# The front end of an encoder kernel is rebuilt: adaLN weights first, tokens turned with scale and shift, twelve early products, one schedule up to the sweeps

## The chip, the cores and the metric

The kernel runs on one core of a Trainium2 chip. A core has five engines: TensorE (PE in the profile) multiplies, VectorE (DVE), ScalarE (ACT) and GpSimd (POOL) do the elementwise work, SyncE (SP) issues transfers. Each engine runs its own instructions in the order in which they were written, and semaphores hold it until what it needs is there. The metric is the time of one execution on the device in microseconds (us), lower is better.

## What is computed

One layer of a hybrid encoder, in float32, on a prompt of 1024 tokens and a sample of 256, each of 1024 features. The 1280 tokens are handled together.

```
def mixer_layer(x, c, w_ada, b_ada, norm_g, w_in, ...):
    mod = c @ w_ada + b_ada                                  # adaLN: c is one row for each sequence
    shift, scale, gate = jnp.split(mod[:, None, :], 3, axis=-1)
    h = rms_norm(x, norm_g) * (1.0 + scale) + shift
    p = h @ w_in                                             # 1024 -> 11280 columns
    cb, cc, cx, cz, q, k, v, o, mz, gpre, gmerge = split_combined(p)
    y_conv = cb * centred_dwconv3(cc * cx, conv_w, conv_b) * jax.nn.silu(cz)
    ...                                                      # two chunkwise mLSTM passes give hm
    y_m = jax.nn.sigmoid(o) * hm * jax.nn.silu(mz)
    g_conv, g_mlstm = jnp.split(jax.nn.sigmoid(gmerge), 2, axis=-1)
    merged = g_conv * (y_conv @ w_proj_conv) + g_mlstm * (y_m @ w_proj_mlstm)
    return x + gate * (merged @ w_out)
```

## The kernel before, in words

**Stages.** The kernel has four: a front end that brings x and the adaLN weights in and makes h with features on the partitions; the long product h @ w_in; the mLSTM sweeps; the merge and the output product. The change is in the first two.

**Front end** (L336 to L458). SP loads eight small tables (L242 to L267), the ten chunks of x of 128 tokens (`xin`, 0.5 MB each), then eight pieces of the adaLN weights (`wa`, 1 MB each) through five buffers, and the first weights of the long product. ACT squares and sums each chunk, DVE makes the inverse root by Newton's steps and scales the chunk by it. PE turns the chunks (80 turns of 128x128, L392), and ACT and DVE alternately copy the results into 16 tiles `xt` of 128 features by 640 tokens. PE multiplies c by the weights (32 matmuls of 4x512, L405, each run as two passes), the result is turned and becomes `s1` and `shf`, a scale and a shift for each feature and sequence (L440). This part is one plan of its own, and its pools are closed behind it. Then `affine` (L849) applies scale and shift to the xt tiles in place.

**The long product.** h is cut into four quarters: B11 and B21 are the lower and the upper half of the features for the first 640 tokens, B12 and B22 for the others. A `Strassen` group takes two times 128 columns of w_in and makes the four results in seven products instead of eight (L527): against B11 (`b00` in the profile), B21 (`b10`), t2, t3, t1 and t4 (in `xt` buffers), B22 (`b11`). Here t3 = B22 - B12, t2 = t3 + B11, t1 = B12 - B11, t4 = B21 - t2, made once by `combine` (L843). Every operand is held as two parts: a rounded high part (ACT's cast) and the rest as low part (a subtraction on DVE or POOL), by `both_parts` (L834) for h and `split_op` (L325) for weights. A product is then high by high, high by low, low by high: 24 matmuls of 128x320, for each of four feature quarters 6. It goes to one of three accumulators (`psX`), from which ACT or DVE adds it to a partial result in a buffer `q` of 640 columns (L606, L618). There are 44 groups, 308 products: 8 groups for the merge gates, 3 for head 0, 8 for the output gates, 16 for the convolution, 9 for the other heads. The first two products of a group need only B11 and B21; in four groups these two, called corners, are made first (`Corner`), while the other operands are still in the making.

**Order.** Nothing is run as it is written down. `op` records each step with its engine, a cost, what it reads and writes and a step number; `Board.order` (L95) sets the order of all recorded steps by letting each engine take the step that can start first, with ties within 0.25 us broken by step number. A step can't be placed before a buffer of its pool is free, and buffers of one kind are given out in the order in which they were recorded. `play` then writes the instructions down. Before the change that happens in several plans, one for each `phase`: the front end; the gates and head 0; the first output gates with the recurrences (`recurrences`, the running maxima and decays of the mLSTM gates, with pool `gt`); the other output gates with the exponentials (`weights`, pool `gw`); the convolution (pool `ab`); the other heads with the adaLN third (`thirds`, pool `gw2`). The ring of q buffers is made anew: eight in the gate plan, five in the middle plans, six in the last. A pool that opens where an older one lay waits until that one's last readers, stores included, are done.

Of the kernel before, what the change touches and what calls it, by code (L numbers as in the profile page):

```python
# [40 lines left out]
class Board:  # L41
# [30 lines left out]
    def op(self, eng, us, f, r=(), w=(), after=(), low=False):  # L72
# [16 lines left out]
        o.bufs = {b for t in (*r, *w) for b in (t if isinstance(t, tuple) else (t,)) if isinstance(b, self.Buf)}  # L89
# [5 lines left out]
    def order(self):  # L95
# [4 lines left out]
        for o in self.ops:  # L100
            o.before = {b for b in o.before if not b.played}
            count[o] = len(o.before)
            for b in o.before:
                after.setdefault(b, []).append(o)
# [25 lines left out]
        while ready:  # L130
            first = None
            can = []
            for o in ready:
                t = begin(o)
                if t is not None:
                    can.append((t, o))
                    if first is None or t < first[0]:
                        first = t, o
# [42 lines left out]
def encoder_kernel(  # L181
# [39 lines left out]
    v_dr = dram.tile([T, D], F32, name="v_dr")  # L221

# [19 lines left out]
    dma(rows[0:8, :], c_prompt.rearrange("a (r p) -> (a r) p", p=P))  # L242
    dma(rows[8:16, :], c_sample.rearrange("a (r p) -> (a r) p", p=P))
    dma(rows[RSH:RSH + 16, :], b_ada[0, 0:2 * D].rearrange("(r p) -> r p", p=P))
    dma(rows[RNG:RNG + 8, :], norm_g.rearrange("a (r p) -> (a r) p", p=P))
    dma(rows[RMH:RMH + 8, :], mh_norm_g.rearrange("a (r p) -> (a r) p", p=P))
    dma(rows[RCW:RCW + 24, :], conv_w.rearrange("a w (r p) -> (a w r) p", p=P))
    dma(rows[RCB:RCB + 8, :], conv_b.rearrange("a (r p) -> (a r) p", p=P))
# [18 lines left out]
    dma(b32[0:16, :], b_gates.rearrange("a s h -> (a s h)").rearrange("(x o) -> x o", o=1))  # L267

    def rsqrt_newton(pool, out, v, n):

        r = pool.tile([P, n], F32, tag="rs_r", name="rs_r")
        t = pool.tile([P, n], F32, tag="rs_t", name="rs_t")
        A.activation(r[:], v, AF.Sqrt, bias=zero[:, 0:1], scale=1.0)
        V.reciprocal(r[:], r[:])
        V.tensor_tensor(out=t[:], in0=r[:], in1=r[:], op=ALU.mult)
        V.tensor_tensor(out=t[:], in0=t[:], in1=v, op=ALU.mult)
        V.tensor_scalar(out=t[:], in0=t[:], scalar1=-0.5, scalar2=1.5, op0=ALU.mult, op1=ALU.add)
        V.tensor_tensor(out=out, in0=t[:], in1=r[:], op=ALU.mult)
# [34 lines left out]
    xp = xstack.enter_context(tc.tile_pool(name="xp", bufs=17))  # L313
    lo_, hi_ = slice(0, TH2), slice(TH2, T)
# [17 lines left out]
    raw_a = {}  # L332

    def corner_split(n, j):
        raw = raw_a[n]
        w = split_op(lambda: raw[:].rearrange("p a (b c) -> p (a b) c", b=2)[:, 4 * j:4 * j + 4, :], [raw])  # L336
        for b in w:
            b.open = True
        raw.open = j == 0
        return w  # L340


    xt = {jl: [buf(xp, [P, TH2], F32, "xt", 17) for _ in range(4)] for jl in ((0, 0), (1, 0), (0, 1), (1, 1))}
    GROUPS = [range(0, 3), range(3, 5), range(5, 8), range(8, 10)]

    with tc.tile_pool(name="xs", bufs=1) as xs, tc.tile_pool(name="ad", bufs=1, side="right") as ad, \
            tc.tile_pool(name="psP", bufs=1, space=PSUM) as psP:
        rst, ssq = (xs.tile([P, NC], F32, name=nm) for nm in ("rst", "ssq"))
        junk = xs.tile([P, D], F32, name="junk")
        xin = [buf(xs, [P, D], F32, "xin", 10) for _ in range(NC)]  # L350
        was = [buf(ad, [P, 2 * D], F32, "wa", 5) for _ in range(KT)]
        pada = [psP.tile([P, 2, 512], F32, name=f"pada{h}") for h in range(2)]
        cz4 = ad.tile([P, KT, 4], F32, name="cz4")
        mod = ad.tile([4, 2 * D], F32, name="mod")
        modT = ad.tile([P, 2, KT, 2], F32, name="modT")

        def load_x(cs):
            for c in cs:
                load(512, lambda c=c: xin[c][:], x_rows(c), (), [xin[c]])

        def norm_x(cs):
            n, s = len(cs), slice(cs[0], cs[-1] + 1)
            sq = [("ssq", c) for c in cs]
            for c in cs:
                op("ACT", 1.35, lambda c=c: A.activation(junk[:], xin[c][:], AF.Square, bias=zero[:, 0:1], scale=1.0,
                                                         accum_out=ssq[:, c:c + 1]), r=[xin[c]], w=["junk", ("ssq", c)])
            op("DVE", .2, lambda: V.tensor_scalar(out=ssq[:, s], in0=ssq[:, s], scalar1=1.0 / D, scalar2=EPS, op0=ALU.mult,
                                                  op1=ALU.add), r=sq, w=sq)
            r, t = (buf(xs, [P, n], F32, f"{nm}{cs[0]}", 1) for nm in ("rr", "rt"))
            op("ACT", .3, lambda: A.activation(r[:], ssq[:, s], AF.Sqrt, bias=zero[:, 0:1], scale=1.0), r=sq, w=[r])  # L370
# [8 lines left out]
            op("DVE", 1.0, newton, r=[*sq, r], w=[r, t, ("rst", cs[0])])  # L379
            for c in cs:  # L380
                op("DVE", .75, lambda c=c: V.tensor_scalar(out=xin[c][:], in0=xin[c][:], scalar1=rst[:, c:c + 1], scalar2=None,
                                                           op0=ALU.mult), r=[xin[c], ("rst", cs[0])], w=[xin[c]])

        def turn_x(i, cs):
            t0, tn = cs[0] * P, len(cs) * P
            for kt in range(KT):
                px = buf(psP, [P, 512], F32, "px", 2)
                dst, d0 = xt[kt // 4, t0 // TH2][kt % 4], t0 % TH2
# [1406 lines left out]
```

## Time and profile before

| | us |
|---|---|
| median of 3 runs (1753.81 to 1754.83) | 1753.84 |
| the profiled execution | 1753.36 |
| its span, first to last instruction | 1751.6 |
| PE busy (96%) | 1686.7 |
| DVE busy (55%) | 957.3 |
| ACT busy (35%) | 611.3 |
| POOL busy (40%) | 693.9 |

In the page's picture of the span in 40 slices, PE is at 5 and 9 tenths in the first two slices of 44 us, at 6 in the third (88 to 131 us), and at 9 or more nearly everywhere behind. Matmuls overlap, so their busy times add up to more than the time between their starts; for the time a product takes, starts are counted instead. The profiled execution's time is 1.76 us longer than its span.

### The profile page before, as it was taken

How to read it: one execution, taken by the hardware profiler on the slowest of the kernel's cores; microseconds unless marked ns; L12 is line 12 of the kernel's file. 1: busy time of each engine (PE TensorE's matmuls, PEld its weight loads, DVE VectorE, ACT ScalarE, POOL GpSimd, SP SyncE). 2: the span in 40 equal slices, each digit the busy share in tenths (PEclk: the TensorE clock that was granted, in tenths of full speed). 3: DMA queues.
4: the chain of work that ended last, by engine and by line, in shares of the span. 5: the costliest groups of instructions: out<-in, count | busy, mean ns of one | idle time of the engine just before them, and what ended most of it. 6: DMA issues, size and time to landing. Idle time of an engine off the chain costs nothing.

```text
span 1751.6 us, 27967 instructions
## 1 busy us (share of the span) xinstructions
PE 1686.7 (96%) x10702; PEld 1596.3 (91%) x10702; DVE 957.3 (55%) x1653; ACT 611.3 (35%) x1201; POOL 693.9 (40%) x511
## 2 busy tenths in 40 slices
PE   5969999999999999999999999999999999999997
PEld 2569999999999999999999999999888889898986
DVE  4496343345564556555565666552147777565645
ACT  5443333223553222222222222222246565433222
POOL 0264333233674466766666533333210001223412
PEclk9979999999999999999999999999999999999999
DMA  8213233221663222112221344335878864684531
GB/s 303 91 59 132 98 101 101 88 80 45 176 180 104 64 79 79 63 56 71 71 67 67 118 137 136 112 121 197 292 238 268 268 219 153 228 278 132 216 120 60
DMA packets 213754, 239.53 MB, mean 137 GB/s; under 512 B 12420, under 2 KB 172404, under 8 KB 212596
## 3 DMA queue, kind: packets, MB, share of 16 engines
q1 hardware_dynamic: 213620, 237.74, 42.0%
q8 instruction: 85, 1.39, 0.3%
q14 instruction: 49, 0.40, 0.1%
HBM read 169.46 MB, written 68.23 MB: 136 GB/s over the span
## 4 chain that ended last, share of the span: by engine, by line
PE 88%; DVE 5%; DMA 3%; issue 2%; ACT 1%; SPq 1%; POOL 0%; DVEq 0%; ACTq 0%; POOLq 0%
PE acc L675 58%; PE qc L1296 3%; PE u L1314 3%; PE accd L1469 2%; PE accd L1470 2%; PE accd L1471 2%; PE accd L1682 2%; PE accd L1683 2%; PE accd L1681 2%; PE pada L405 2%; PE acc L1537 2%; PE acc L1536 2%; PE acc L1538 2%; DVE xt L846 1%; PE misc L810 1%
## 5 line engine op out<-in xcount | busy, mean ns | idle before, releaser
L606 DVE TENSOR_TENSOR q<-acc,q 128x640 f32<-128x640 f32 x292 | 236.7, 821 | 337.0 <-PE acc L675 333.0
L329 POOL TENSOR_TENSOR wl<-comb,wh 128x512 fp32r<-128x512 f32 x176 | 240.6, 1369 | 303.1 <-ACT wh L328 274.1
L329 POOL TENSOR_TENSOR wl<-raw,wh 128x512 fp32r<-128x512 f32 x136 | 182.2, 1340 | 249.2 <-ACT wh L328 246.1
L675 PE MATMUL acc<-xt,wh 128*128 128x320 f32 x1408 | 265.7, 311 | 1.2 <-POOL xt L841 1.2
L675 PEld LDWEIGHTS acc<-xt,wh 128*128 128x128 f32 x1408 | 221.8, 189 | 1.7 <-POOL xt L841 1.4
L328 ACT CAST wh<-comb 128x512 fp32r<-128x512 f32 x176 | 108.5, 619 | 209.7 <-PE acc L675 188.8
L328 ACT CAST wh<-raw 128x512 fp32r<-128x512 f32 x136 | 83.9, 620 | 272.6 <-PE acc L675 214.0
L675 PE MATMUL acc<-xt,wl 128*128 128x320 f32 x704 | 161.1, 310 | 0.0
L1497 POOL TENSOR_TENSOR wl<-raw,wh 128x512 fp32r<-128x512 f32 x28 | 36.4, 1301 | 234.0 <-ACT wh L1496 233.5
L675 PEld LDWEIGHTS acc<-xt,wl 128*128 128x128 f32 x704 | 118.2, 189 | 0.1
L495 ACT ACTIVATE q<-q,zero 128x640 f32<-128x640 f32 x80 | 66.4, 830 | 90.4 <-DVE q L606 87.8
L559 DVE TENSOR_TENSOR comb<-raw 128x512 f32<-128x512 f32 x88 | 78.8, 896 | 31.1 <-DMA raw<-in_w_in_dram 19.8
L675 PE MATMUL acc<-t2H,wh 128*128 128x320 f32 x352 | 83.1, 318 | 8.4 <-ACT t2H L840 7.2
L675 PE MATMUL acc<-t2L,wh 128*128 128x320 f32 x352 | 82.4, 316 | 5.1 <-DVE t2L L841 5.1
L675 PE MATMUL acc<-t2H,wl 128*128 128x320 f32 x352 | 82.4, 316 | 4.0 <-POOL wl L329 4.0
L559 DVE TENSOR_TENSOR comb<-raw,comb 128x512 f32<-128x512 f32 x44 | 46.0, 1045 | 72.5 <-POOL wl L329 72.5
L675 PE MATMUL acc<-b00H,wh 128*128 128x320 f32 x352 | 81.5, 313 | 2.2 <-ACT b00H L840 2.2
L675 PE MATMUL acc<-b11H,wh 128*128 128x320 f32 x352 | 81.8, 313 | 0.6 <-DVE q L606 0.6
L1469 PE MATMUL accd<-y,wh 128*128 128x320 f32 x256 | 79.5, 310 | 2.8 <-DVE og L1447 1.5
L675 PE MATMUL acc<-b00L,wh 128*128 128x320 f32 x352 | 81.0, 311 | 0.3 <-DVE b00L L841 0.3
L675 PE MATMUL acc<-b10H,wh 128*128 128x320 f32 x352 | 80.9, 311 | 0.0
L675 PE MATMUL acc<-t3H,wh 128*128 128x320 f32 x352 | 80.7, 311 | 0.0
(281 smaller groups left out, 4188.9 us busy)
## 6 DMA issues: line engine op xcount, KB each, us to landing
raw<-in_w_in_dram SPq DMA_DIRECT2D x96, 256.0 KB
raw<-in_w_in_dram SPq DMA_DIRECT2D x44, 512.0 KB
th_dr<-q SPq DMA_DIRECT2D x32, 320.0 KB
th<-th_dr SPq DMA_DIRECT2D x32, 320.0 KB
wa<-in_w_ada_dram SPq DMA_DIRECT2D x8, 1024.0 KB
raw<-in_w_proj_conv_dram SPq DMA_DIRECT2D x16, 512.0 KB
k<-kn_dr SPq DMA_DIRECT2D x64, 128.0 KB
raw<-in_w_proj_mlstm_dram SPq DMA_DIRECT2D x16, 512.0 KB
```

The lines of the kernel that those rows point to most:

```text
L328: op("ACT", .63, lambda: A.copy(wh[:], src()), r=r, w=[wh])
L329: op("POOL", 1.4, lambda: G.tensor_tensor(out=wl[:], in0=src(), in1=fp(wh[:]), op=ALU.subtract), r=[*r, wh], w=[wl])
L405: op("PE", .88, lambda h=h, j=j: PE.matmul(pada[h][0:4, j, :], cz4[:, kt, :], was[kt][:, h * D + j * 512:h * D + (j + 1) * 512], start=kt ...
L495: A.activation(out, in_, AF.Tanh, bias=zero[:, 0:1], scale=0.5)
L559: op("DVE", .9, lambda: V.tensor_tensor(out=t[:], in0=x(), in1=y(), op=o), r=[x.tok, y.tok], w=[t])
L606: op("DVE", .82, lambda: V.tensor_tensor(out=two(dst()), in0=acc[:, :, 0:TQ], in1=two(t()), op=ALU.add), r=[acc, t.tok], w=[dst.tok])
L675: PE.matmul(acc[:, q, 0:TQ], st_[:, k_, :], m_[:, q * TQ:(q + 1) * TQ], start=k_ == 0 and n == 0, stop=k_ == 3 and n == 2)
L1296: PE.matmul(pq[:, 0:HD + 2], qTs[i][:, kd, c * P:(c + 1) * P], C[:, kd, :], start=kd == 0, stop=kd == 1)
L1314: PE.matmul(pu[:, db, 0:HD + 2], k[:, db * P:(db + 1) * P], wv[:], start=True, stop=True)
L1469: PE.matmul(accs[q][:, :TQ], wh, yH, start=kt == 0, stop=False)
L1470: PE.matmul(accs[q][:, :TQ], wh, yL, start=False, stop=False)
L1497: op("POOL", 1.36, lambda wh=wh, wl=wl, src=src: G.tensor_tensor(out=wl[:], in0=src(), in1=fp(wh[:]), op=ALU.subtract), r=[raw, wh], w=[wl])
```

## The change

The front end is no plan of its own any more, and all that runs up to the sweeps is recorded into one plan, with one `play`. Its transfers are planned at 330 KB a microsecond instead of 230.

- The eight small loads are issued by ACT, and SP starts with the adaLN weights. These and x lie in the buffers that later hold the operands b00, b10, b11, t2 and t3. The order of loads is: five pieces of wa, weights of the first corner, three pieces of wa, x chunks 0 to 3, two more corner weights, x chunks 4 to 9, each of which waits for its place if a wa piece stood there.
- PE multiplies c by the adaLN weights first. The copy out of PSUM behind a turn applies scale and shift (`turn_x`), so `affine` is gone, and x is turned for 640 tokens at a time.
- Six groups instead of four have their corners made early: twelve products instead of eight. The first results of four of these groups lie in two large buffers, those of two go to memory (`p1_dr`) and are read back.
- All low parts of the operands, and all combinations, are made by DVE. Before, POOL made two of the low parts of B21, two of t3, the four of t1, and the four combinations t1.
- One pool `rp` with five q buffers and two buffers `big` of 1280 columns serves all: corners, gate inputs, the recurrences' small tiles (both `big` and one q, held from the first step to the last), the exponentials, the convolution's u and cv, the adaLN third.
- Each PE step of the recurrences is two products later than the one before it.

The core of the diff:

```
-    dma(rows[0:8, :], c_prompt.rearrange("a (r p) -> (a r) p", p=P))
+    A.dma_start(rows[0:8, :], c_prompt.rearrange("a (r p) -> (a r) p", p=P))
...
+    psX = pstack.enter_context(tc.tile_pool(name="psX", bufs=1, space=PSUM))
...
+    rp = rstack.enter_context(tc.tile_pool(name="rp", bufs=1, side="right"))
...
+    quarter("b11", hp, "b00", (((0,), ()), ((1,), ())))
+    quarter("b21", hp, "b10", (((2,), ()), ((3,), ())))
+    quarter("b22", hp1, "b11", (((4,), (4, 5)), ((5,), (6, 7))))
+    quarter("t2", sp, "t2", (((6,), (8,)), ((7,), (9,))))
+    quarter("t3", sp, "t3", (((), (0, 1)), ((), (2, 3))))
...
+    def beginning():
...
+        def turn_x(cs, kts):
...
+                if kt % 2 == (cs[0] in (3, 5)):
+                    op("ACT", .2 + .1 * len(cs), lambda px=px, dst=dst, d0=d0, sc=sc, sh=sh: A.activation(
+                        dst[:, d0:d0 + tn], px[:, :tn], AF.Identity, bias=sh, scale=sc), r=[px, "s1"], w=[(dst, int(d0 > 0))])
+                else:
+                    op("DVE", .17 + .13 * len(cs), lambda px=px, dst=dst, d0=d0, sc=sc, sh=sh: V.tensor_scalar(
+                        out=dst[:, d0:d0 + tn], in0=px[:, :tn], scalar1=sc, scalar2=sh, op0=ALU.mult, op1=ALU.add),
+                       r=[px, "s1"], w=[(dst, int(d0 > 0))])
...
+        for kt in range(5):
+            load_wa(kt)
+        corner_load(0)
+        for kt in range(5, KT):
+            load_wa(kt)
+        for c in range(4):
+            load_x(c)
+        corner_load(2)
...
+        for cs in GROUPS[:2]:
+            norm_x(cs)
+        early.update({(n, j): corner_split(n, j) for j in range(2) for n in (0, 2)})
+        for kt in lows:
+            board.step = kt - 6
+            for cs in GROUPS[:2]:
+                turn_x(cs, [kt])
+            both_parts("b11", B11, [kt])
...
+        for k in range(12):
...
     def qtile():
-        return buf(ring[0], [P, TH2], F32, "q", ring[1])
+        return buf(rp, [P, TH2], F32, "q", 5)
+
+    def big():
+
+        return buf(rp, [P, T], F32, "big", 2)
...
-    def recurrences(gt):
+    def recurrences():
+
+        places = [big(), big(), qtile()]
...
+                if eng == "PE":
+                    board.step += 2
-                op(eng, us, f, r=["pre", *r], w=["pre", *w])
+                op(eng, us, f, r=["pre", *r], w=["pre", *w, *places])
...
-    for n, j in ((0, 0), (2, 0), (0, 1), (2, 1), (4, 0), (4, 1), (6, 0), (6, 1)):
+    for n, j in ((0, 0), (2, 0), (0, 1), (2, 1), (4, 0), (4, 1), (6, 0), (6, 1), (8, 0), (8, 1), (10, 0), (10, 1)):
...
-            phase(ends[9])
+    advance(ends[9])
...
+    board.KB_US = 330.0
+    board.play()
+    board.KB_US = Board.KB_US
+    rstack.close()
```

PE's first instructions before: `px` is the PSUM tile of a turn, `pada` that of the adaLN product, `wa` and `xin` the loaded weights and x.

```order
L251 MATMUL misc<-ident,rows 128x80
L392 MATMUL px<-ident,xin 128x128 x46
L405 MATMUL pada_143<-wa,cz_145 4x512
L392 MATMUL px<-ident,xin 128x128 x3
L405 MATMUL pada_143<-wa,cz_145 4x512
L392 MATMUL px<-ident,xin 128x128 x6
```

And now, where L473 is the adaLN product into `acc`, L489 the turn of its result, L442 the turn of x into `misc`, L748 a product (b00 against the high and low parts wh and wl of a weight):

```order
L252 MATMUL misc<-ident,rows 128x80
L473 MATMUL acc<-b00H,big 4x512 x4
...
L473 MATMUL acc<-t2L,big 4x512 x4
L489 MATMUL misc<-ident,comb 128x4 x16
L442 MATMUL misc<-ident,t3H 128x128 x2
L442 MATMUL misc<-ident,t3L 128x128 x2
L442 MATMUL misc<-ident,b11H 128x128
...
L748 MATMUL acc<-b00H,wh 128x320 x2
L748 MATMUL acc<-b00L,wh 128x320 x2
L748 MATMUL acc<-b00H,wl 128x320 x2
```

The adaLN products went ahead of all turns of x; 15 turns stand between them and the first product, the other 65 among the first products.

PE at the last three matmuls of the recurrences before (L1000 and L1001 turn the running maxima, L1033 broadcasts the states), with twelve rows of products between the second and the third:

```order
L675 MATMUL acc<-t3H,wl 128x320 x2
L1000 MATMUL misc<-ident,cm 128x128
L1001 MATMUL misc<-ident,am 1x128
L675 MATMUL acc<-t3H,wh 128x320 x2
L675 MATMUL acc<-t3L,wh 128x320 x2
L675 MATMUL acc<-t3H,wl 128x320 x2
...
L675 MATMUL acc<-xt,wl 128x320 x2
L1033 MATMUL misc<-st_3397,ones 128x160
```

And now (L1082 is the former L1001, L1114 the former L1033):

```order
L748 MATMUL acc<-t2H,wh 128x320 x2
L748 MATMUL acc<-t2L,wh 128x320 x2
L748 MATMUL acc<-t2H,wl 128x320 x2
L1082 MATMUL misc<-ident,big 1x128
L1114 MATMUL misc<-big,ones 128x160
L748 MATMUL acc<-t3H,wh 128x320 x2
```

The two last matmuls of the recurrences now follow each other with no product between them; the t3 product behind them is the fourth of the second output-gate group.

ACT behind the exponentials of the recurrences (L1137, the former L1056) now: L565 is a tanh on a q buffer, L679 the copy of a group's first product out of its accumulator.

```order
L328 CAST wh<-comb 128x512
L1137 ACTIVATE gcol<-gcol,zero 128x80 x3
L1137 ACTIVATE decay<-decay,zero 128x80
L565 ACTIVATE q<-q,zero 128x640 x2
L679 COPY q<-acc 128x640
```

Two tanh and the copy stand directly behind the exponentials; before, tanh and weight casts took turns there, and the copy came six rows behind them.

## Rows read from the trace of the kernel before

**Rows 1.** Matmuls of products by stage: us, PE busy (starts), clock, DMA.

```profile
66.70:135.00 68.30, 54.51 (x315) 0.83 0.17 58
...
376.00:396.00 20.00, 15.50 (x89) 0.83 0.35 99
...
474.00:976.00 502.00, 502.00 (x3425) 1.00 0.27 81
976.00:1000.00 24.00, 19.47 (x118) 0.86 0.52 170
```

**Rows 2.** The timeline: start, length, engine, line, operation, idle before, releaser.

```profile
42.71 20.76 PE L405 MATMUL pada<-wa,cz 128*4 128x512 f32 x48
...
66.75 0.56 PE L675 MATMUL acc<-b00H,wh 128*128 128x320 f32 x2 [2.18 <-ACT b00H L840]
```

**Rows 3.** The timeline of the first 10 us.

```profile
0.74 0.40 SPq L242 DMA_DIRECT2D rows<-in_c_prompt_dram  x1
...
3.62 3.89 SPq L317 DMA_DIRECT2D xin<-in_x_prompt_dram  x8
...
5.45 0.18 DVE L411 COPY cz<-cols 128x16 f32<-128x16 f32 x1
7.46 1.28 ACT L365 ACT_TABLE_LOAD   x1 [7.46 <-DMA xin<-in_x_prompt_dram]
```

**Rows 4.** All engines by stage: PE, PEld, DVE, ACT, POOL busy, clock, DMA.

```profile
12.00:14.00 2.00, 0.00 (x0) 0.00 (x0) 0.17 (x1) 1.97 (x4) 0.00 (x0) 1.00 1.02 418
...
70.00:72.00 2.00, 2.00 (x9) 2.00 (x9) 1.88 (x5) 1.79 (x3) 0.00 (x0) 0.50 0.00 0
```

**Rows 5.** The timeline of norm, turn, eviction, cast.

```profile
10.02 1.15 ACT L365 ACTIVATE junk<-xin,zero 128x1024 f32<-128x1024 f32 x1
...
11.29 1.15 ACT L365 ACTIVATE junk<-xin,zero 128x1024 f32<-128x1024 f32 x1
...
13.85 0.30 ACT L370 ACTIVATE rr<-ssq,zero 128x3 f32<-128x3 f32 x1
...
15.18 2.08 DVE L381 TENSOR_SCALAR xin<-xin,rst 128x1024 f32<-128x1024 f32 x3
...
32.57 0.88 PE L392 MATMUL px<-ident,xin 128*128 128x128 f32 x6
...
65.97 1.98 ACT L840 CAST b00H<-xt 128x640 fp32r<-128x640 f32 x3
```

**Rows 6.** Tile `xt` (min/median/max ns), groups by line, timeline of splits.

```profile
L846 DVE TENSOR_TENSOR xt<-xt x12: 811/1990/2185, 88.9 to 120.6; 128x640 f32<-128x640 f32 x12
...
L846 DVE TENSOR_TENSOR xt<-xt 128x640 f32<-128x640 f32 x12 | 20.1, 1714 | 0.0
...
L606 DVE TENSOR_TENSOR q<-acc,q 128x640 f32<-128x640 f32 x292 | 236.7, 821 | 337.0 <-PE acc L675 333.0
...
123.52 1.27 POOL L329 TENSOR_TENSOR wl<-comb,wh 128x512 fp32r<-128x512 f32 x1 [3.54 <-ACT wh L328]
```

**Rows 7.** The timeline of the recurrences' last steps.

```profile
394.46 0.27 PE L1001 MATMUL misc<-ident,am 128*1 128x128 f32 x1
...
396.75 0.23 DVE L1030 TENSOR_TENSOR st<-st,amr 1x80 f32<-1x80 f32 x1
...
399.05 0.53 PE L1033 MATMUL misc<-st,ones 1*128 1x160 f32 x2
400.83 0.23 DVE L1051 TENSOR_TENSOR decay<-mg 128x80 f32<-128x80 f32 x1
...
402.00 0.82 ACT L495 ACTIVATE q<-q,zero 128x640 f32<-128x640 f32 x1
```

**Rows 8.** PE's waits from 135 to 1245 us: total, times, longest.

```profile
PE acc L675 <- POOL wl L329: 4.0, 2, 3.8
```

**Rows 9.** The chain that ended last: start, length, what.

```profile
376.12 2.37 DMA qT_dr<-q
...
991.07 1.07 PE misc L810 x5
```

More of the change, by code (lines that the diff above doesn't have):

```diff
@@ L346, in encoder_kernel @@
[L346 to L359, printed above, removed]
+        return split_op(lambda: raw[:].rearrange("p a (b c) -> p (a b) c", b=2)[:, 4 * j:4 * j + 4, :], [raw])
@@ new lines, in encoder_kernel, with both_parts @@
+    GROUPS = [range(0, 3), range(3, 5), range(5, 8), range(8, 10)]
+    def both_parts(nm, src, ks=range(4)):
+        for i in ks:
+            hi, lo = (MOV[nm][part][i] for part in range(2))
+            bh, bl = (MOV_B[nm][part][i] for part in range(2))
+            x = src[i]
+            op("ACT", .73, lambda hi=hi, x=x: A.copy(hi(), x[:]), r=[(x, 0), (x, 1)], w=[bh])
+            op("DVE", .83, lambda hi=hi, lo=lo, x=x: V.tensor_tensor(out=lo(), in0=x[:], in1=fp(hi()), op=ALU.subtract),
+               r=[(x, 0), (x, 1), bh], w=[bl])
@@ L390, in turn @@
                 def turn(px=px, kt=kt):
                     for j, c in enumerate(cs):
-                        PE.transpose(px[:, j * P:(j + 1) * P], xin[c][:, kt * P:(kt + 1) * P], ident[:])
-                op("PE", .11 * len(cs), turn, r=[xin[c] for c in cs], w=[px])
-                f = (A.copy, V.tensor_copy)[kt % 2]
-                op(("ACT", "DVE")[kt % 2], .5, lambda f=f, px=px, dst=dst, d0=d0: f(dst[:, d0:d0 + tn], px[:, :tn]),
-                   r=[px], w=[(dst, i)])
-        def load_ada(kt):
-            load(1024, lambda: was[kt][:], wada[:, kt, 0:2 * D], (), [was[kt]])
@@ L480, in encoder_kernel @@
-    for nm, pool, tag in (("b11", hp, "b00"), ("b21", hp, "b10"), ("b22", hp1, "b11"), ("t2", sp, "t2"), ("t3", sp, "t3")):
-        quarter(nm, pool, tag)
-    ring = [None, 8]
+            V.tensor_copy(shf[:], modT()[:, 0])
+        op("DVE", .8, modulation, r=[(pm, h, j) for h in range(2) for j in range(2)], w=["s1", (junk, "m")])
+        B11, B21, B12, B22 = (xt[jl] for jl in ((0, 0), (1, 0), (0, 1), (1, 1)))
+        lows, highs = range(4), range(4, 8)
+        board.step = -6
+        for cs in GROUPS[:2]:
+            norm_x(cs)
@@ L1175, in encoder_kernel @@
[L1175 to L1188 removed]
+    beginning()
@@ L1190, in first_y @@
+    advance(ends[0] - 10)
+    board.step = at[0]
+    gate_inputs()
+    advance(ends[0])
+    board.step = at[0]
+    recurrences()
+    for n in range(KT):
+        if n > 1:
+            for i in range(NH * NC // 2):
+                if i * 6 // (NH * NC // 2) == n - 2:
+                    board.step = at[0] + 7 * (i * 6 % (NH * NC // 2)) // (NH * NC // 2)
+                    weights(i)
+        advance(ends[n + 1])
+    advance(ends[9])
     def first_y():
```

552 lines of the change are left out of this document (261 added, 291 removed).

## The prediction

> **What bounds the kernel now.** I read the table by stages first, then the line of the products in it, then the stretch up to 135 us in order of time. TensorE is the bound. A product is 24 matmuls of 128x320, and in the undisturbed stretch from 474 to 976 us 3425 of them start in 502 us, one every 0.1466 us [rows 1]; a product is 3.52 us. So a stage has lost time by as much as it is longer than its matmuls times 0.1466, less the PE's other work in it. From the first product at 66.75 us [rows 2] to 135 us there are 315 matmuls, 46.2 us of work in 68.3: 22.1 us lost. From 376 to 396 us there are 89, 13.1 us, beside some 2 us of nine small recurrence matmuls like those of [rows 7]: about 5 lost. From 976 to 1000 us there are 118, 17.3 us, beside five token turns of 1.1 us [rows 9]: 5.6 lost [rows 1]. Ahead of 66.75 us no product runs. Only these four places can give anything to this change. The sweeps and the output stage keep their instruction order, and I count them at nothing; what hides an edit in them is that there is none.
>
> **The first product, 66.75 us before.** What comes ahead of it is x (10 loads), its norm and turn, the 32 adaLN products, the shift and scale, the affine pass, the split. Now wa is loaded first, the products start with it, and x is handled beside them.
> Start: the first x load, issued at 3.62 us, let ACT start at 7.46 us, so 3.84 us for 0.52 MB, of which 1.25 us is transfer at the 418 GB/s of the following loads, and 2.6 us latency [rows 3, 4]. The first wa load has 1.05 MB, 2.5 us of transfer, and SP issues it at about 0.7 us, where the first small load stood [rows 3]: it lands at 5.8 us. The column vector, which before was ready at 5.6 us [rows 3], still comes from the small loads, now issued by ACT beside that traffic; I take 6.5 us for both.
> The adaLN products: 48 passes took 20.76 us at full clock [rows 2], 0.4325 each, 64 passes 27.7 us. The loads bring 1.05 MB in 2.5 us, PE uses it in 3.46, so PE sets the pace. PE comes from idleness: where the products began after 66.75 us, the granted clock was 0.50 (1.2 GHz) in 70 to 72 us [rows 4]; I add 1.6 us, half of about 3.2 us. The last pass ends at P = 35.8 us.
> After P, x chunks 0 to 9 are there or landing (8.4 MB of wa, 5.2 MB of x and three 0.5 MB pieces at 418 GB/s end by about 41 us), but ACT has little of the norm behind it. By ACT's and DVE's order after P: a copy 0.6, the fourth square 1.27 (squares start 1.27 apart [rows 5]), the root 0.3, Newton's steps 1.0 (from the root's end to the scalings at 15.18 us), three scalings 2.1 [rows 5]; beside them POOL has three weight splits of 1.27 us [rows 6], which I let hold DVE for 2.7. That is P+8.0. Then the second group: 0.2, root 0.4, Newton 1.0; ACT goes on with the first eviction 0.5, three more squares 3.8 and the first cast 0.66 (its row has three) [rows 5], which ends at about P+14, while DVE (two scalings, turns, an eviction) is there at P+12. I take P+13 = 48.8 us for the first product. The bounds are P+11.8 with no hold by POOL and P+16 with x late. **-18.0 us** (-22 to -14).
>
> **From there to the 17th product.** Twelve early products (six column pairs against two quarters of the tokens) replace eight, so 42 us of PE work cover the making of t1 to t4 instead of 28. In this stretch PE also has 65 of the 80 token turns, 0.14 us each (six took 0.88 [rows 5]): 9 us; and half clock at its start, 2 us. Products alone would bring PE to the 17th at 2 + 9 + 16 x 3.52 = 67.3 us after the first.
> DVE must have made the operands by then, and now makes all of them; before, POOL took 12 of these operations. By the order, the last turns of the second token half stand behind 20 quarter products of 0.88 us: 2 + 9 + 17.6 = 28.6 us after the first product. From there DVE has, up to the last low part of t4, 39 two-operand passes of 0.81 us (the shortest of their row; three are weight combinations) and five additions of 0.82: 35.7 us [rows 6]. Three additions, one combination, a cast and a split of the weights for the 17th follow, 5.3 us. Undisturbed, PE would wait 28.6 + 35.7 + 5.3 - 67.3 = 2.3 us.
> But POOL still splits weights, one split a product, some 11 in that time. The 12 combinations L846 took 20.1 us, not 9.7: each of them waited for POOL, with a median of 1.99 us [rows 6]. So 11 splits of 1.27 us cost DVE between 0 and 14 us; I take 10, near the upper end, because DVE is never idle in that stretch.
> The Trainium skill (SBUF — State Buffer, Who interferes with whom) says that a DVE instruction with two SBUF inputs and a GpSimd instruction that reads SBUF exclude one another for a whole instruction. The rows agree with that; by the rule alone the hold would be the full 14 us, and without it nothing, which is 4 us more or 10 less than I use.
> Lost time is then 2 + 9 + 12.3 = 23.3 us against 22.1: **+1.2 us** (-9 to +5).
>
> **The recurrences.** One ring of five 640-column buffers and two of 1280 now serves everything up to the sweeps; before, the gate stage had eight, the recurrences their own pool. Now they hold one of the five and both large ones until their last step. An output-gate group needs five at its fifth product (u2, o, u3, the result, its tanh), so that tanh waits for the recurrences, and behind it the copy that empties the accumulator of the next group's first product. There are three accumulators, so PE gets three products further and stops. The order shows it: the last two recurrence matmuls stand next to each other, where before twelve rows of products lie between, and ACT has the two tanh and the copy right behind the exponentials. The wait, from the rows of before [rows 7]: PE's transpose and the DVE chain, 394.46 to 396.98, 2.5 us; the broadcast matmul, 0.6; DVE from that matmul's end, 399.58, to 401.06, 1.5; exponentials to the tanh at 402.00, 1.0; DVE's last scaling with its hand-off 0.3; two tanh of 0.82 and two DVE passes of 0.82, with hand-offs 3.7; the copy, as a cast of that width, 0.8. Together 10.4 us, and 2.6 us for a clock that falls to 0.5 after such a pause: 13.0 against 5.0 before. **+8.0 us** (+2 to +10).
>
> **From the convolutions to the heads.** There POOL stood at the clearing of an accumulator that waited for a store from the pool being closed, with the weight splits behind it; PE waited up to 3.8 us for a split [rows 8]. Now that clearing stands some steps earlier, between the multiplications, and no pool closes. **-5.6 us** (-5.6 to 0); if the shared large buffers make another such wait, it comes back here.
>
> The rest comes to nothing: two spilled products go to memory and back (2.4 us for a store [rows 9], products ahead of their use), the small loads on ACT, where it is idle, the roots' table load ahead of the first square.
>
> Sum: -18.0 + 1.2 + 8.0 - 5.6 = -14.4 us. On the profiled execution's 1753.36 us (span 1751.6, 1.76 outside) that is 1739.0; the median of the runs lies 0.5 above it, so **1739 us**.
>
> **Rivals.**
> A, DVE keeps ahead and the recurrences end in time. POOL's splits come early, as its order has all twelve early splits ahead of those of combinations, and DVE has slack; or ACT and DVE reach the recurrences' end before PE is three products further. For it: undisturbed, only 2.3 us are missing. Against it: the row of L846. Price: 10 us less on DVE, 1 on the first product, 6 of the 8: about 1722 us.
> B, the front doesn't move as far: a load of x waits for the wa that stands in its place, and the norm of ten chunks falls behind P on ACT and DVE. If the first product comes at 61 us, 12 later, the gain is 3 us: 1751, no change. For it: three 0.5 MB pieces with 512-byte runs stand ahead of the fifth chunk. Against it: by the loads' bytes all of x is there by 41 us, and ACT gets to the fifth square only at about 40.
> C, slower: five buffers starve the gate and head groups, which had eight and six (20 groups of 44). A buffer is free again only after its store has landed, 2.4 us [rows 9]. If half a landing shows in every group, 20 x 1.2 = 24 us, the time is 1763 us; from 0.75 us a group on it eats the gain. Against it: the output-gate and convolution groups ran on five all along, with no loss in 502 us [rows 1]. For it: the recurrence shows that one buffer less than five stops the chain.
> That the early products don't come early at all is B at its worst.
>
> **Numbers.** The forecast with its mechanism 0.52 (own range 1728 to 1750), A 0.24, B 0.12, C 0.12. About 0.2%, 3.5 us, is what a measurement of this kernel can tell from no change. Faster: nearly all of the forecast, A, and a little of B, 0.78; same 0.11; slower 0.11. The range reaches into A and to the edge of C: 1721 to 1757 us.
>
> **What would show it.** In the trace after: first product at 47 to 52 us; the adaLN passes one after the other from about 6.5 to 36 us; between the first and the 17th product a wait of PE for low parts made by DVE, with DVE's two-operand passes over 1.2 us on average; one wait of 8 to 13 us of PE for ACT right behind the recurrences' broadcast matmul, and no wait of that kind before the heads. If PE never waits for DVE there, the hold was mis-sized; if the products run more than 0.1466 us apart in the gate stage, C was right.

## The result, and the profile after

The changed kernel takes 1740.62 us in the median of four runs (1740.05 to 1741.99), against 1753.82 before; the ratio is 0.9929, with a 95% interval of 0.9912 to 0.9946. Forecast were 1739 us. The profiled execution has a span of 1738.6 us against 1751.6, 13.0 less. So the sum came out near. Several of its terms did not, and the experiments show which.

The line of the products in the table by stages, kernel after (us, PE busy and starts of matmuls, PEld, granted clock, DMA share, GB/s), answers to [rows 1]:

```profile
376.00:438.00 62.00, 52.88 (x339) 52.14 (x338) 0.92 0.32 92
...
474.00:976.00 502.00, 502.00 (x3426) 502.00 (x3425) 1.00 0.27 81
976.00:1000.00 24.00, 19.90 (x131) 18.92 (x130) 1.00 0.54 171
```

The undisturbed stretch has 3426 starts, as before 3425: a product still takes 3.52 us. The loss around the recurrences (first row) has grown, though: 339 matmuls, and in the same window of the kernel before:

```profile
376.00:438.00 62.00, 57.10 (x371) 56.16 (x370) 0.94 0.21 64
```

PE's waits after, over the whole span (engine, line and releaser; total, times, longest):

```profile
PE misc L442 <- DVE t3H L429: 6.0, 2, 5.8
PE acc L748 <- ACT q L679: 5.4, 1, 5.4
PE acc L473 <- DMA b00H<-in_w_ada_dram: 5.2, 1, 5.2
...
PE acc L748 <- DVE t2L L383: 3.1, 2, 2.1
PE misc L1114 <- DVE big L1111: 3.0, 1, 3.0
PE acc L748 <- ACT wh L328: 2.9, 1, 2.9
PE misc L878 <- DVE q L665: 2.5, 1, 2.5
PE acc L932 <- DVE q L920: 2.3, 1, 2.3
```

From top to bottom: the turns wait for the norm, the recurrences (5.4 and 3.0), the first adaLN load, the operands before the 17th product (3.1 and 2.9), the convolutions' end (2.5), and one wait that the prediction doesn't have: the gate projection at L932.

A wait doesn't tell what it costs in the end. That is told by the same product's start in both timelines:

| Place | before, us | after, us | after less before |
| --- | --- | --- | --- |
| first product | 66.75 | 54.60 | -12.15 |
| early stage over (products on `b11`) | 216.1 | 203.1 | -13.0 |
| first product behind the gate projection | 337.3 | 328.3 | -9.0 |
| behind the recurrences | 421.6 | 417.8 | -3.8 |
| 45 us further on, in the weights' stretch | 466.5 | 460.0 | -6.5 |
| head products, first turns done | 994.5 | 984.1 | -10.4 |
| first of the sweeps' products on `qT` (L1296, after L1332) | 1242.5 | 1232.0 | -10.5 |
| the last of them | 1485.3 | 1472.9 | -12.4 |
| end of the span | 1751.6 | 1738.6 | -13.0 |

The front gives 13 us, the gate projection and the recurrences take 9 of them back, and the later stages give 9 again.

### The profile page after: what moved, and what is told of

Its sections match the earlier page's. It is cut to its first block, busy times and chain, and to the rows that moved or that the text cites. A ratio compares the mean times of both kernels' runs of the same rounds, so it can differ in the third digit from the quotient of the medians.

```text
span 1738.6 us, 27963 instructions
## 1 busy us (share of the span) xinstructions
PE 1678.7 (97%) x10702; PEld 1590.9 (92%) x10702; DVE 962.9 (55%) x1653; ACT 607.8 (35%) x1189; POOL 674.0 (39%) x499
## 4 chain that ended last, share of the span: by engine, by line
PE 90%; DVE 5%; issue 2%; DMA 2%; ACT 1%; POOL 0%; ACTq 0%; SPq 0%; DVEq 0%; POOLq 0%
PE acc L748 60%; PE qc L1332 3%; PE u L1350 3%; PE accd L1506 2%; PE accd L1505 2%; PE accd L1507 2%; PE accd L1718 2%; PE accd L1719 2%; PE accd L1717 2%; PE acc L1572 2%; PE acc L1573 2%; PE acc L1574 2%; PE acc L473 2%; PE misc L878 1%; PE misc L1393 1%
## 5 line engine op out<-in xcount | busy, mean ns | idle before, releaser
L665 DVE TENSOR_TENSOR q<-acc,q 128x640 f32<-128x640 f32 x272 | 220.9, 822 | 318.4 <-PE acc L748 314.5
L748 PE MATMUL acc<-xt,wh 128*128 128x320 f32 x1408 | 264.6, 310 | 0.0
L748 PEld LDWEIGHTS acc<-xt,wh 128*128 128x128 f32 x1408 | 220.6, 188 | 0.4
L748 PE MATMUL acc<-xt,wl 128*128 128x320 f32 x704 | 160.4, 309 | 0.0
L748 PEld LDWEIGHTS acc<-xt,wl 128*128 128x128 f32 x704 | 117.7, 188 | 0.0
L815 POOL TENSOR_TENSOR big<-big,q 128x640 f32<-128x640 f32 x48 | 86.7, 1806 | 47.6 <-DVE q L665 40.5
L565 ACT ACTIVATE q<-q,zero 128x640 f32<-128x640 f32 x76 | 63.2, 831 | 69.8 <-DVE q L665 68.8
L748 PE MATMUL acc<-t3H,wh 128*128 128x320 f32 x352 | 81.5, 313 | 5.4 <-ACT q L679 5.4
L748 PE MATMUL acc<-b11H,wh 128*128 128x320 f32 x352 | 82.2, 314 | 2.9 <-ACT wh L328 2.9
L748 PE MATMUL acc<-t2L,wh 128*128 128x320 f32 x352 | 80.1, 309 | 3.1 <-DVE t2L L383 3.1
L748 PE MATMUL acc<-b00H,wh 128*128 128x320 f32 x352 | 82.3, 314 | 0.0
L748 PE MATMUL acc<-t3L,wh 128*128 128x320 f32 x352 | 81.3, 313 | 0.0
L748 PE MATMUL acc<-t3H,wl 128*128 128x320 f32 x352 | 81.0, 312 | 0.0
L748 PE MATMUL acc<-t2H,wh 128*128 128x320 f32 x352 | 81.0, 311 | 0.0
```

What stands on the lines that cost most here:

```text
L565: A.activation(out, in_, AF.Tanh, bias=zero[:, 0:1], scale=0.5)
L665: op("DVE", .82, lambda: V.tensor_tensor(out=two(dst()), in0=acc[:, :, 0:TQ], in1=two(t()), op=ALU.add), r=[acc, t.tok], w=[dst.tok])
L748: PE.matmul(acc[:, q, 0:TQ], st_[:, k_, :], m_[:, q * TQ:(q + 1) * TQ], start=k_ == 0 and n == 0, stop=k_ == 3 and n == 2)
L815: op("POOL", 1.65, lambda: G.tensor_tensor(out=dst(), in0=dst(), in1=t(), op=ALU.mult), r=[dst.tok, t.tok], w=[dst.tok])
```

## The experiments

All edits are to the changed kernel; the times are medians, the ratios are to the kernel before, run on the same chip. Runs of one kernel lie up to 6 us apart, so where an effect is that small I go by the starts in the profile.

**The first load.** The prediction let SP issue the first adaLN load at 0.7 us. The timeline of the kernel after shows otherwise; it answers to [rows 2, 3]:

```profile
4.72 0.37 PE L252 MATMUL misc<-ident,rows 80*128 80x80 f32 x1 [4.72 <-DMA rows<-in_conv_b_dram]
...
5.12 0.39 SPq L317 DMA_DIRECT2D b00H<-in_w_ada_dram  x1
...
5.57 0.17 DVE L458 COPY big<-cols 128x16 f32<-128x16 f32 x1
...
10.26 5.80 PE L473 MATMUL acc<-b00H,big 128*4 128x512 f32 x8 [5.17 <-DMA b00H<-in_w_ada_dram]
...
36.50 3.60 PE L473 MATMUL acc<-t2L,big 128*4 128x512 f32 x8
...
54.60 0.88 PE L748 MATMUL acc<-b00H,wh 128*128 128x320 f32 x2
```

The load goes out 0.03 us after PE has read `rows` (4.72 + 0.37). `rows` lies in a pool that is closed right after that matmul, and the operand pool `hp`, opened next on the same side, takes its memory. The instruction order says so too: this load waits for seven small loads and for PE. SP's waits up to 60 us:

```profile
SPq L317 <- DMA rows<-in_norm_g_dram: 2.7, 1, 2.7
...
SPq L317 <- PE misc L252: 0.5, 1, 0.5
```

Would it help to free the load? The pieces change places, so that the first four go to pools that don't touch `rows`:

```
-    quarter("b11", hp, "b00", (((0,), ()), ((1,), ())))
-    quarter("b21", hp, "b10", (((2,), ()), ((3,), ())))
-    quarter("b22", hp1, "b11", (((4,), (4, 5)), ((5,), (6, 7))))
-    quarter("t2", sp, "t2", (((6,), (8,)), ((7,), (9,))))
+    quarter("b11", hp, "b00", (((4,), ()), ((5,), ())))
+    quarter("b21", hp, "b10", (((6,), ()), ((7,), ())))
+    quarter("b22", hp1, "b11", (((0,), (4, 5)), ((1,), (6, 7))))
+    quarter("t2", sp, "t2", (((2,), (8,)), ((3,), (9,))))
```

> The first adaLN weights go to b11 and t2, not to b00 and b10, which lie where the small rows lay; nothing else changes. Theory 1 (the first load waits for memory that the small rows still occupy, and all that follows is late by it): SP issues it at about 0.7 us instead of 5.12, the adaLN passes start at 6 to 6.5 us instead of 10.26 and end at about 36 instead of 40.1; the first product comes 3.5 to 4 us earlier, at about 51, and the time falls by as much, to about 1737 us. Rival (the loads of x or DVE's queue set the first product, not the adaLN passes): the passes move, the first product moves by less than 1 us, 1740 us.

1741.12 us (0.9931, 0.9914 to 0.9947): no gain, but not as the rival had it, since the passes themselves didn't move. Its timeline:

```profile
2.14 0.33 SPq L317 DMA_DIRECT2D b11L<-in_w_ada_dram  x1
...
5.86 0.33 SPq L317 DMA_DIRECT2D t2H<-in_w_ada_dram  x1
...
9.31 0.37 PE L252 MATMUL misc<-ident,rows 80*128 80x80 f32 x1 [9.31 <-DMA b11L<-in_w_ada_dram]
...
10.37 6.08 PE L473 MATMUL acc<-b11H,big 128*4 128x512 f32 x8 [0.70 <-DVE big L458]
```

The weights are there early, and now the small rows are late: read at 9.31 us instead of 4.72, behind two large loads (2.1 MB, issued at 0.74 and 2.14 us; the other two left SP only at 5.86 and 6.24, when all loads of `rows` had been issued). The wait turned from the one operand to the other. With only one load let ahead, pieces 0 and 4 trading places:

```
-    quarter("b11", hp, "b00", (((0,), ()), ((1,), ())))
+    quarter("b11", hp, "b00", (((4,), ()), ((1,), ())))
...
-    quarter("b22", hp1, "b11", (((4,), (4, 5)), ((5,), (6, 7))))
+    quarter("b22", hp1, "b11", (((0,), (4, 5)), ((5,), (6, 7))))
```

> Of the adaLN weights only the first 1.05 MB goes to memory that is free from the start (b11), so that SP issues it at about 0.7 us; the second, as in the changed kernel, waits until the small rows are read. Theory 1 (with 4.2 MB ahead of them the rows came at 9.31 us, with 1.05 MB they come after about a quarter of that delay, 5.8 to 7 us): the adaLN passes start at 6.5 to 7.5 us instead of 10.26 and end 1 to 3 us earlier, at 37 to 39; the norm behind them follows, and the time falls by 1 to 3 us, to about 1738.5. Rival (the rows come behind any early load, and the second adaLN load so much later that PE waits for it): the last pass ends at 40 or later, 1740 to 1742.

1739.32 us (0.9913, 0.9899 to 0.9928; the interval overlaps that of the changed kernel, so the profile has to tell). Its timeline:

```profile
0.74 0.38 SPq L317 DMA_DIRECT2D b11H<-in_w_ada_dram  x1
...
6.87 0.36 PE L252 MATMUL misc<-ident,rows 80*128 80x80 f32 x1 [6.87 <-DMA b<-in_b_gates_dram]
...
7.93 6.00 PE L473 MATMUL acc<-b11H,big 128*4 128x512 f32 x8 [0.70 <-DVE big L458]
```

The passes start 2.3 us earlier, the first product at 52.5, 2.1 earlier, and the shift of 2 us is still there at the sweeps (1222.0 against 1224.0). So the first product does follow the adaLN passes, and about 2 of the missing 3.8 us of the start could be had; the small rows, now read 2.15 us later (6.87 for 4.72), set the start.

**Behind the last pass.** The planner is told that loads are faster, which puts two squares and a root ahead of the evictions:

```
-    board.KB_US = 330.0
+    board.KB_US = 400.0
```

> The planner reckons 400 instead of 330 KB/us for loads, which puts the third and fourth square of x and the first root ahead of ACT's evictions of the adaLN sums. Theory 1 (behind the last adaLN pass the norm on ACT and DVE sets the first product: two squares of 1.2, a root, Newton's steps of 3.1 held by three GpSimd splits, scalings): these steps fall in the 5.2 us in which ACT waits for the last passes, and the first product comes 5 to 6 us earlier, at about 49; what follows up to the 17th product on DVE moves with it, and the time falls to 1735 or 1736 us. Rival (the second token half on DVE sets the 17th product whatever the first does): first product earlier, the time within 1.5 us of 1740.

1737.72 us (0.9903, 0.9885 to 0.9921), span 1734.2, 4.4 less. Its timeline:

```profile
34.83 1.15 ACT L412 ACTIVATE big<-t3L,zero 128x1024 f32<-128x1024 f32 x1
...
35.98 0.28 ACT L417 ACTIVATE rr<-ssq,zero 128x3 f32<-128x3 f32 x1
...
37.10 0.16 DVE L424 TENSOR_TENSOR rst<-rt,rr 128x3 f32<-128x3 f32 x1
...
49.68 0.88 PE L748 MATMUL acc<-b00H,wh 128*128 128x320 f32 x2
```

In the kernel after, the root stood at 41.76 and Newton's last step ended at 45.13; here at 35.98 and 37.26. The first product comes 4.9 us earlier, the 17th 7.6 (123.05 against 130.69): theory 1. The median is 2.9 us lower, though, not the 5 expected. Of the 7.9 us gained at the gate projection's end (320.2 for 328.1) 4.4 are left in the span; 3.3 go into a wait of PE for DVE's additions at 440 to 480 us, in the weights' stretch, which the kernel after doesn't have.

**Up to the 17th product.** Four early products fewer:

```
-    for n, j in (..., (6, 0), (6, 1), (8, 0), (8, 1), (10, 0), (10, 1)):
+    for n, j in (..., (6, 0), (6, 1)):
...
-        for k in range(12):
-            if k in (0, 2, 4):
+        for k in range(8):
+            if k == 0:
...
-        at[0] = 12
+        at[0] = 8
```

> Eight early products instead of twelve, all else as in the changed kernel; the four others come in their groups. Theory 1 (DVE's making of the operands sets when the products after the early ones can start, and four more early products give PE 14.1 us to do in that time): PE waits some 10 to 14 us longer between the first product and 140 us, and the time rises to 1750 to 1755 us. Rival (DVE is not what sets it, and the early products only change places): 1740 to 1742 us.

1751.72 us (0.9983, 0.9973 to 0.9993): 11 us lost, in the range of theory 1. PE's waits for products from 60 to 140 us in this kernel:

```profile
PE acc L748 <- ACT t2H L382: 8.3, 1, 8.3
PE acc L748 <- DVE xt L383: 3.0, 1, 3.0
```

With a third of 0.7 us they come to 12.0 us, against 6.4 in the kernel after: 5.6 longer, not 10 to 14. The clock gives some of the rest: behind the long wait, from 104 to 108 us, it is 0.50 again. The 30th product starts 8.5 us later than in the kernel after (190.5 against 182.0), the first of the sweeps 8.3. So the direction and the time are theory 1's, and its wait was too long. DVE and ACT make the operands in their own time, and the four products fill it or leave it empty. With eight early products little of the change's gain is left.

Is it GpSimd that makes DVE slow there? In the next kernel the low parts of the early weights are cleared, not computed, so the early products lack that term.

```
-        op("POOL", 1.4, lambda: G.tensor_tensor(out=wl[:], in0=src(), in1=fp(wh[:]), op=ALU.subtract), ...)
+        part = (lambda: G.tensor_tensor(...)) if low else (lambda: G.memset(fp(wl[:]), 0.0))
+        op("POOL", 1.4, part, ...)
```

> The low parts of the early products' weights are cleared by GpSimd instead of made by a subtraction, so these products lack that term; the order stays. Theory 1 (GpSimd's subtractions hold DVE's passes with two operands): between the first and the 17th product the passes fall to 0.81 to 0.83 us on average (16 of 0.998 before), DVE has 8 to 11 us less to do there, PE's waits of 3.1 us for the low parts of t2 and 2.9 for a weight cast shrink by half or more, and the time falls by 3 to 6 us, to about 1736. Rival (the passes are long for another reason): they stay near 1.0, and the time at 1740.

DVE's groups from the first to the 17th product, kernel after (busy, mean ns):

```profile
L388 DVE TENSOR_TENSOR xt<-xt 128x640 f32<-128x640 f32 x16 | 15.5, 998 | 0.2
L383 DVE TENSOR_TENSOR xt<-xt 128x640 fp32r<-128x640 f32 x8 | 6.3, 818 | 0.3
...
L383 DVE TENSOR_TENSOR t3L<-xt,t3H 128x640 fp32r<-128x640 f32 x4 | 4.6, 1188 | 0.0
L383 DVE TENSOR_TENSOR t2L<-xt,t2H 128x640 fp32r<-128x640 f32 x4 | 4.4, 1089 | 0.0
L383 DVE TENSOR_TENSOR b11L<-xt,b11H 128x640 fp32r<-128x640 f32 x4 | 4.2, 1086 | 0.0
```

and with the cleared parts, in the same stretch (its line numbers are one higher):

```profile
L389 DVE TENSOR_TENSOR xt<-xt 128x640 f32<-128x640 f32 x16 | 13.5, 872 | 0.2
...
L384 DVE TENSOR_TENSOR t2L<-xt,t2H 128x640 fp32r<-128x640 f32 x4 | 5.5, 1365 | 0.4 <-ACT t2H L383 0.4
...
L384 DVE TENSOR_TENSOR b11L<-xt,b11H 128x640 fp32r<-128x640 f32 x4 | 3.1, 818 | 0.0
L384 DVE TENSOR_TENSOR t3L<-xt,t3H 128x640 fp32r<-128x640 f32 x4 | 3.1, 816 | 0.0
```

Passes that had a subtraction on GpSimd beside them fall from 1.19 and 1.09 to 0.82 us. Those of `t2` become longer, 1.37: two of the four have a subtraction for a later product's weights beside them, which this kernel still has, and take 1.91 us each. So the hold follows the subtractions, and passes beside a clearing, which reads nothing, stay at 0.82 us. The gain is smaller than expected: the 44 passes with two operands go from 0.99 to 0.89 us on average, 4.4 us in all and not 8 to 11. PE's wait for the low parts of t2 falls from 3.1 to 1.2 us, but that for the weight cast ahead of the 17th product stays as it was (2.85 us in both), so GpSimd's hold doesn't make that one. The time is 1737.42 us (0.9911, 0.9894 to 0.9927); the first product comes 2.0 us earlier (52.6), the 17th 6.0 (124.74), the first sweep 3.7. In the profiled execution the sweeps then took 3.1 us more; they vary by that much by themselves (below).

**The recurrences.** They hold two large buffers and one of the five small ones. Counting the columns that they ask for gives 1841, which fit in the two large ones of 1280; first fit never reaches the third. It is held for nothing:

```
-        places = [big(), big(), qtile()]
+        places = [big(), big()]
...
-                self.i = next(i for i in range(3) if used[i] + n <= (T, T, TH2)[i])
+                self.i = next(i for i in range(2) if used[i] + n <= T)
```

> The recurrences hold the two large buffers and no longer a 640-column one; their 1841 columns fit in two of 1280. Theory 1 (the fifth buffer stops the output-gate group, and through its tanh and the accumulators PE): PE no longer waits 3.0 us ahead of the broadcast matmul and 5.4 us for ACT's copy, the stretch around the recurrences loses about 7 us in 62 as before instead of 11.7, and the time falls by 4 to 5 us, to about 1736 us. Rival (the tanh is late because ACT and DVE are occupied by the recurrences' own steps): the wait for the copy stays at about 5 us, 1740.6 us.

1730.08 us (0.9868, 0.9853 to 0.9883): 10.5 less, twice what was expected. First what the kernel after does at the recurrences' end; it answers to [rows 7]:

```profile
402.32 0.27 PE L1082 MATMUL misc<-ident,big 128*1 128x128 f32 x1
...
405.55 0.51 PE L1114 MATMUL misc<-big,ones 1*128 1x160 f32 x2 [2.95 <-DVE big L1111]
...
408.01 0.20 DVE L1140 TENSOR_SCALAR gcol<-gcol 128x80 f32<-128x80 f32 x1 [0.48 <-ACT gcol L1137]
408.13 0.81 ACT L565 ACTIVATE q<-q,zero 128x640 f32<-128x640 f32 x1
...
409.84 0.83 ACT L565 ACTIVATE q<-q,zero 128x640 f32<-128x640 f32 x1 [0.89 <-DVE q L568]
...
410.70 0.69 ACT L679 COPY q<-acc 128x640 f32<-128x640 f32 x1
...
411.44 0.90 PE L748 MATMUL acc<-t3H,wh 128*128 128x320 f32 x2 [5.39 <-ACT q L679]
```

The tanh at 408.13 stands right behind the exponentials in ACT's order. In the plan the last scaling frees the buffer for it; on the chip it doesn't wait for that scaling, which ends only at 408.21, since no data lie in the third place. The buffer acts through the order alone. Behind the tanh come the second tanh and the copy, and PE waits for the copy. PE's granted clock there, windows of 4 us:

```profile
404.00:408.00 4.00, 0.51 (x2) 0.91 0.00 0
408.00:412.00 4.00, 0.56 (x2) 0.50 0.55 115
412.00:416.00 4.00, 4.00 (x17) 0.50 0.48 182
```

From the pause on the engine has the lower of its two levels, 1.2 GHz (0.50), up to 416 us. Without the third place, the window that had 339 matmuls:

```profile
376.00:438.00 62.00, 61.45 (x415) 60.60 (x415) 1.00 0.33 100
```

76 more, 76 x 0.1466 = 11.1 us. That is also 44 more than before the change: the loss of the kernel before around its recurrences was not inherent either. With five buffers the planner puts products between the recurrence's matmuls, and PE never waits.

**The gate projection.** The unforeseen wait, in DVE's timeline of the kernel after:

```profile
315.13 0.82 DVE L665 TENSOR_TENSOR q<-acc,q 128x640 f32<-128x640 f32 x1 [2.69 <-PE acc L748]
315.88 1.05 DVE L919 CAST q<-big 128x128 fp32r<-128x128 f32 x1
316.96 0.29 DVE L920 TENSOR_TENSOR q<-big,q 128x128 fp32r<-128x128 f32 x1
```

Its split weights now lie in one of the five small buffers, so the cast stands behind the last addition of the group, and PE, done at 315.1, starts at 317.40. Then it runs at half clock for part of the way (0.63 from 318 to 320 us, 0.52 from 320 to 322): the matmuls on `b00` and `b10` take 0.35 to 0.40 us on average, those on `b11` 0.31. Together 4.0 us, the step from -13.0 to -9.0 in the table. In a weight-combination buffer instead:

```
-        a, w = places[0], buf(rp, [P, TH2], F32R, "q", 5)
+        a, w = places[0], buf(cp, [P, 4, P], F32R, "comb", 5)
```

> The gate projection's split weights stand in a combination buffer instead of one of the five 640-column buffers. Theory 1 (their split waits for that ring, behind the last addition of the group ahead): PE no longer waits 2.3 us for it, the following matmuls don't run at half clock (1.7 us), and the time falls by 4.0 us, to 1736.6. Rival A (their load is late): the wait stays, 1740.6. Rival B (one combination buffer less makes the weight combinations late): PE waits for splits elsewhere, above 1742.

1737.13 us (0.9909, 0.9895 to 0.9924), 3.5 us less for the 4.0 expected. The wait and the half clock are gone: the gate projection ends at 325.7 instead of 328.1. That is 2.4 us, not 4.0, since in this profile PE ran at half clock longer behind its wait at the 17th product (last section). At the sweeps 1.8 us are left. Both edits:

> The recurrences without the 640-column buffer and the gate projection's weights in a combination buffer, together. Theory 1 (two separate waits): no wait of PE between 140 and 976 us over 1 us; 2 to 4 us below the version without the buffer alone (1730.1), so 1726 to 1728. Rival (what the second gives is lost again at the recurrences, where DVE's chain ends when it ends): 1730.

1728.90 us (0.9852, 0.9837 to 0.9868). From 140 us up to the heads no wait of PE over 1 us is left; the first one, of 2.5 us, is that for the turn of the first head product (L878), which ends at 967.6 us here. The median lies 1.2 us below the one edit alone, less than expected, and the intervals overlap, so the times don't show what the wait was worth. The starts show it in one profile each: the 30th product comes 1.3 us later than with the one edit (181.9 against 180.6), the 70th 1.2 us earlier (337.0 against 338.2), so 2.5 us are gained between them.

**Everything together.**

> These two edits with the planner's loads at 400 KB/us. Theory 1 (the front's gain of the earlier squares stays, since nothing behind it takes it back): as much below the two edits alone as the planner's number alone is below the changed kernel, some 5 us, so about 1722. Rival (it is lost before the 17th product): as the two edits alone, 1727.

1721.61 us (0.9809, 0.9793 to 0.9824): 7.3 below the two edits alone, 32 below the kernel before. PE's waits in it from 145 to 1200 us, all of them:

```profile
PE misc L878 <- DVE q L665: 2.2, 1, 2.2
PE acc L1572 <- ACT wh L328: 1.0, 1, 1.0
```

The wait at 440 to 480 us, which took 3.3 us of the planner's number alone, isn't there. Two tries to go further:

> The same edit on top of the two buffer edits with the loads at 400 KB/us. If the last adaLN pass sets the first product there, it comes 1 to 3 us earlier than 49.9 and the time is about 1719.5; if x sets it (its loads come behind the same bytes), the time is that of the version without it, 1721.6, within 1 us.

1723.19 us (0.9820, 0.9805 to 0.9835): the same. The last pass ends 1.9 us earlier, the first product only 0.5 (49.4): there x sets it, since ACT waits for x's fifth block up to 39.4 us.

> The two buffer edits with the loads reckoned at 450 KB/us, above what they reach in the trace (about 420). The order puts a square and a cast of the second group ahead of ACT's evictions of the adaLN sums too. If what arrives sets the pace there, these steps stand in the way: first product 0 to 2 us later than 49.9, 1721.6 to 1724; if ACT still has idle time there, up to 1 us earlier, 1720.5.

1736.38 us (0.9900, 0.9883 to 0.9916), a clear miss: 15 us lost. At the first product it is 1.9 us late, as expected. The rest is far behind it, in the waits from 440 to 700 us:

```profile
PE acc L748 <- DVE q L665: 8.6, 3, 4.5
```

A number that only the front was thought to feel re-orders the whole plan, and 450 brought waits far behind the front. 400 is what happened to suit this plan, not a rule.

## Why the prediction was right or wrong

The forecast missed by 1.6 us, and that is luck. In the profile its terms were off by +5.9 us (first product), -2.1 (to the 17th), +4.0 (gate projection), -2.8 (recurrences), -2.7 (behind them), +1.7 (convolutions to heads) and -2.6 (sweeps and end): +1.4 in all. Of the signs that were to show it, the wait for low parts made by DVE came (3.1 us for t2), and the wait for ACT behind the broadcast matmul; no sign with a number fell within its limits.

*The first product: -12.15 for -18.0, outside its range.* The step that failed is the start. "SP issues it at about 0.7 us" took the place in the queue for the time of issue; the load waited for the memory of the rows until 5.12. The 5.1 us from there to the first pass are the 2.5 and 2.6 that the prediction had. So of the 5.8 us that are missing, 3.8 are the start; 0.5 is slow passes at the beginning (half of the first eight took 1.03 us or more, the later ones 0.59; the granted clock listed for 10 to 12 us is 1.00, so it doesn't show why), and 1.5 the way from the last pass's end at 40.1, 14.5 for 13. The prediction's own steps ended at 14 on ACT and at 12 on DVE; it took 13, where the later of the two sets. On that way Newton's steps and three scalings took 6.1 us beside GpSimd's splits (42.07 to 48.21), for 5.8; that a square and the root needn't stand there at all, the planner's number showed.

*To the 17th product: 76.1 us for 79.6.* The mechanism is right and its size near. DVE's 44 passes with two operands (the groups above and two more, of 1.04 and 0.82) took 0.99 us on average instead of 0.815, 7.6 more, the five weight combinations 1.1 more, and three scalings of x that fell into this stretch 1.6: 10.3 for the 10 assumed, though the mean stayed under the 1.2 that was to show it. (Not each of the 12 combinations L846 before was held, as the prediction reads them: the shortest took 0.811 us.) PE, which began 5.8 us late, waited 6.0 us for operands and splits instead of 12.3, and the 17th product, forecast for 128.4, came at 130.7. The late front isn't lost in that: where an edit moved the first product, the 17th moved with it, 2.0 us for 2.1 with one load let ahead and 7.6 for 4.9 with the planner's number. The two errors had opposite signs; against the kernel before, the term is -0.85 for +1.2.

*The gate projection: +4.0, for which there was no term.* It was rival C's mechanism, five buffers that starve a group, at one place; the rival looked for it in the gate and head groups, where the spacing of 0.1466 shows none. The prediction listed what held the small buffers and left out that the projection's weights had moved into one.

*The recurrences: +5.2 for +8.0.* Named in kind and place: one wait of 5.4 us for ACT behind the broadcast matmul, with 3.0 ahead of it, and the tanh behind the recurrences' last steps. In the window of 62 us, products leave 12.3 us against 7.6 before; without 2 us for the recurrences' own matmuls 10.3 against 5.6, for 13.0 against 5.0 forecast: the wait was sized too long; its 0.3 for the last scaling isn't there. And the prediction took for given that the third buffer is needed: without it the loss is gone.

*Behind them, -2.7, and the sweeps, -1.9, for nothing.* The weights' stretch lost 2.7 us before and not after; 1.8 of them were two waits of PE for DVE's additions, and no run isolates what removed them. The planner's number alone brought a wait of 3.3 us there. The sweeps' order is the same in all kernels, and from their first to their last product they took 250.8 us before, 248.9 after, and 248.9 to 252.0 in the experiments, so I read this as no effect of the change.

*Convolutions to heads: -3.9 for -5.6.* The wait for GpSimd's split [rows 8] is gone, and 2.5 us came back as a wait for DVE's weight combinations, three of 1.8 to 2.0 us beside GpSimd's splits and multiplications.

Rivals: A needed DVE ahead; it was late. B had the first product at 61, the forecast at 48.8: it came between them. C was right at two places, not in every group.

## What to carry to other kernels

A place at the head of a queue is no time of issue: look at what the instruction waits for, and above all at whose memory its target lies in. When a ring of buffers is shared by more users, list every holder with its first and last instruction, and count what each really uses; here one of five was held by nobody's data and cost 10 us. A sum that comes out near says little of its terms: compare the start of the same product in both timelines, stage by stage.

## What was not expected of the hardware

Small loads beside large ones came later: the rows were read at 4.72 us with no large load issued, 6.87 with 1.05 MB issued at the same time as the first of them, and 9.31 with another 1.05 MB issued among them. That is 2.2 and 2.4 us more, for loads that take 2.5 us each at 418 GB/s. A DVE operation on 128x3 elements took 1.24 us (L423) beside a GpSimd split and 0.17 without: the Trainium skill (SBUF — State Buffer, Who interferes with whom) counts `tensor_scalar` among the operations that can enter a mode of two ports and then exclude GpSimd, and the pair of numbers agrees. And after the same wait of 2.85 us ahead of the 17th product the granted clock from 132 to 136 us was 0.72 in the kernel after and 0.50 in the one with the gate weights moved (then 0.80 up to 140, against 1.00): 20 and 14 matmuls in the first 4 us, 29 and 24 in the next, 11 fewer, 1.6 us.
